# The row of reciprocals in a decoder step's RMS norms: products of a step-zero column with the identity in place of diagonal matrices

## The chip, the cores and the metric

The kernel runs on one core of a Trainium2 chip, as one launch. The metric is the device time of that launch in microseconds. Engines are named as in the profile: PE (TensorE's matmuls), PEld (its loads of a stationary operand, which run ahead of matmuls), DVE (VectorE), ACT (ScalarE), POOL (GpSimd) and SP (SyncE, which issues the DMAs here).

## The reference

One inference step of a decoder of two layers, for a prompt of 1024 tokens and for 8 x 8 sample tokens with their caches. The model width is 1024. Each layer has a mixer (layer 0: gated linear attention beside a convolution module; layer 1: dilated sliding-window attention beside a gated MLP) and a convolutional feed-forward network of 2 x 2816 columns; each of these four parts stands between two RMS norms.

```python
def rmsnorm(x, g):
    x32 = x.astype(jnp.float32)
    y = x32 * lax.rsqrt(jnp.mean(x32 * x32, axis=-1, keepdims=True) + EPS)
    return (y * g.astype(jnp.float32)).astype(x.dtype)
...
def trunk(x, ...):
    for layer in range(DEPTH):
        h = rmsnorm(x, p['norm_pre_mix'][layer])
        ...
        x = x + rmsnorm(y, p['norm_post_mix'][layer])
        h = rmsnorm(x, p['norm_pre_ffn'][layer])
        f, fb = conv_ffn(h, ffn_buf[layer], p['w_up'][layer], ...)
        x = x + rmsnorm(f, p['norm_post_ffn'][layer])
```

## The kernel before

**Layout and halves.** Activations lie transposed: the 1024 features on 8 tiles of 128 partitions, the tokens along the free dimension. The tokens are worked on in two halves. Half A has 512 tokens (4 blocks of 128); half B has 576 (4 blocks of 128 and the 64 sample tokens). A matrix product of half A has 512 moving columns, one of half B two pieces of 288.

**Products.** Each fp32 operand is split into a rounded part and a rest, and a product is three passes: `g<-hi,whi`, `g<-lo,whi` and `g<-hi,wlo`. A weight chunk is loaded as `raw`, ACT writes `whi`, DVE subtracts to get `wlo` (both with three buffers). `g` is a PSUM tile; ACT copies it out, or DVE adds it to `y`.

**A norm.** In the transposed layout a token's sum of squares runs over partitions. So PE multiplies the summed squares with a column of ones (`m<-ones,ss`), which gives one column per block of 128 tokens, with the tokens on partitions. DVE scales it (`r<-m`, L201, in `rstd`), POOL raises it to the power -1/2 (`r<-r,mhalf`, L236). The result `r` has a token on each partition, but the tiles to be scaled have tokens along the free dimension. `rb` turns the column into a row that is the same on all 128 partitions: for each block DVE writes a diagonal matrix `dg` (L201) and PE multiplies it with a matrix of ones (L230), which sums each column and so repeats the diagonal's values on every partition. ACT copies the PSUM tile to `rb` (L207); eight DVE operations `y<-y,vec,rb` (L198) scale the eight tiles; each is then split into `hi` (ACT) and `lo` (DVE), and the next matrix product reads these. `dg` has two buffers, so the third diagonal of a half can be written only when the first product has read its own.

There are 15 calls of `rb` in a launch (eight norms, each for two halves; half B's last one is done in another layout). The eight calls of half A have 4 blocks each, the seven of half B 5 blocks, which makes 67 diagonals and 67 products. In the trace each fp32 product is two matmul instructions and two loads. A name such as `m<-dg,ones` gives the output, then the moving operand, then the stationary one.

**The order of work.** The code issues work in program order, but a scheduler of the framework, which simulates a timeline, puts each engine's instructions in the order in which they are to run; an engine then keeps this order. So a change in a few instructions can move others on all engines. The matrix products of the other half, or of the part before, fill PE while a norm's chain runs.

Of the kernel before, what the change touches and what calls it, by code (L numbers as in the profile page):

```python
# [9 lines left out]
F32 = mybir.dt.float32  # L10
# [3 lines left out]
ALU = mybir.AluOpType  # L14
# [4 lines left out]
P = 128  # L19
# [119 lines left out]
class Kern:  # L139
# [292 lines left out]
    def rb(self, h, ss, r=None):  # L432

        nb = len(h.blocks)
        if r is None:
            ps = self.psn()
            for b, (c0, sz) in enumerate(h.blocks):
                for i, t in enumerate(ss):
                    self.mm(ps[:sz, b:b + 1], t[:, c0:c0 + sz], self.ones[:, :1], i == 0, i == len(ss) - 1)
            r = self.rms(h, ps)  # L440
        rb = self.np_.tile([P, h.n], F32, tag="rb", name=self.nm("rb"), bufs=1)
        for part in ([0, 1, 2, 3], [4]):
            if part[0] >= nb:
                continue
            pb = self.psn()
            for b in part:
                c0, sz = h.blocks[b]
                dg = self.np_.tile([P, P], F32, tag="dg", name=self.nm("dg"), bufs=2)
                self.ts(dg[:sz, :sz], self.ident[:sz, :sz], r[:sz, b:b + 1], 0.0, ALU.mult, ALU.add)
                o0 = c0 - h.blocks[part[0]][0]  # L450
                self.mm(pb[:, o0:o0 + sz], self.ones[:sz, :], dg[:sz, :sz], True, True)
            c0 = h.blocks[part[0]][0]
            w = sum(h.blocks[b][1] for b in part)
            self.acopy(rb[:, c0:c0 + w], pb[:, :w])
        return rb
# [8 lines left out]
    def pre_steps(self, h, xt, ss, name, l, out, r=None):  # L464
        rb = self.rb(h, ss, r)
        yield 1.0
        for k in range(KT):
            self.stt(xt[k], xt[k], self.v(name, l * KT + k), rb, ALU.mult, ALU.mult)
            out.append(self.split(h, xt[k]))
            yield 1.0  # L470

    def post_steps(self, h, y, ss, xs, name, l, xnew, out):
        xl = [self.at(h, [P, h.n], name="xl") for _ in range(KT)]
        for k in range(KT):
            self.dma(xl[k], xs[k])
        rb = self.rb(h, ss)
        yield 1.0
        ss2 = None
        for k in range(KT):
            self.stt(y[k], y[k], self.v(name, l * KT + k), rb, ALU.mult, ALU.mult)  # L480
            self.tt(y[k], y[k], xl[k], ALU.add)
            if xnew is not None:
                if ss2 is None:
                    ss2 = []
                self.sq_add(h, ss2, y[k], k)
                self.dma(xnew[k], y[k])
            yield 1.0
        out.append(ss2)
# [1532 lines left out]
```

## Time and profile before

| | |
|---|---|
| median of 3 runs | 2666.02 us (2665.92 to 2673.85) |
| profiled execution | 2670.34 us |
| its span | 2668.6 us |
| PE busy | 2572.5 us (96%) |
| DVE busy | 1750.3 us (66%) |
| ACT busy | 1210.0 us (45%) |
| POOL busy | 305.4 us (11%) |
| mean granted clock of TensorE | 0.979 |

The span is that of the trace; the profiled execution's own time has 1.7 us around it. Busy time of PE is modelled from overlapping instructions, so its share says how little of the span PE was without work, not how close it is to its peak. The granted clock is a share of 2.4 GHz.

### The profile page before, as it was taken

The page shows a single profiled execution, that of the slowest core. Times are in us where ns is not written, and L with a number is a line of the kernel's source. Part 1 is how long each engine was busy: PE and PEld are TensorE (multiplying, and loading weights), DVE is VectorE, ACT ScalarE, POOL GpSimd, SP SyncE. Part 2 cuts the span into 40 slices and gives each one's busy share as a digit, 9 for nine tenths or more (in the row PEclk, how much of TensorE's full clock was granted, in tenths as well). Part 3 has the DMA queues.
Part 4 walks back from the last instruction along what each step waited for, and adds up shares of the span by engine and source line. Part 5 has one row for each costly group of instructions (what it writes and reads, how often), then busy time and mean ns, then how long its engine had stood idle before and what let it go on. Part 6 is the DMA issues. An engine that isn't in the chain of part 4 may idle for free.

```text
span 2668.6 us, 43691 instructions
## 1 busy us (share of the span) xinstructions
PE 2572.5 (96%) x16481; PEld 2302.2 (86%) x16481; DVE 1750.3 (66%) x3298; ACT 1210.0 (45%) x2330; POOL 305.4 (11%) x594
## 2 busy tenths in 40 slices
PE   7999999999999999999999999889999898999998
PEld 6789788887888789999999889878877678999998
DVE  4888479999677546455558774666654478455556
ACT  5343455443455344535445452235552545434444
POOL 0100001201100001201204020010011112001100
PEclk9999999999999999999999999999998899999999
DMA  6433364455545544232332447875534154322232
GB/s 215 134 107 104 103 229 144 133 173 175 171 138 166 174 143 129 80 110 60 92 120 90 139 132 213 244 215 155 145 105 129 48 176 128 103 88 72 76 90 84
DMA packets 505002, 355.80 MB, mean 133 GB/s; under 512 B 29547, under 2 KB 461282, under 8 KB 504015
## 3 DMA queue, kind: packets, MB, share of 16 engines
q1 hardware_dynamic: 504791, 353.01, 44.1%
q8 instruction: 130, 2.13, 0.3%
q14 instruction: 81, 0.66, 0.1%
HBM read 306.43 MB, written 75.97 MB: 143 GB/s over the span
## 4 chain that ended last, share of the span: by engine, by line
PE 82%; DVE 6%; DMA 6%; ACT 3%; issue 2%; SPq 1%; POOL 0%; DVEq 0%; POOLq 0%; ACTq 0%
PE g L230 74%; PE m L230 6%; PE m L222 2%; DMA kc<-qr 2%; DVE wlo L195 1%; DVE y L198 1%; SPq L186 1%; DMA raw<-in_w_up 1%; ACT whi L207 1%; DMA kc<-in_cache_c_w 1%; DVE cv L198 1%; DVE y L195 1%; DMA raw<-in_w_down 1%; DVE w L195 0%; ACT S L210 0%
## 5 line engine op out<-in xcount | busy, mean ns | idle before, releaser
L230 PE MATMUL g<-hi,whi 128*128 128x288 f32 (+2 forms) x4440 | 1271.5, 334 | 20.4 <-ACT hi L207 6.2
L230 PE MATMUL g<-lo,whi 128*128 128x288 f32 (+2 forms) x4440 | 1264.7, 331 | 8.1 <-DVE lo L195 8.1
L230 PE MATMUL g<-hi,wlo 128*128 128x288 f32 (+1 forms) x4416 | 1251.0, 331 | 0.4 <-DVE wlo L195 0.4
L230 PEld LDWEIGHTS g<-hi,whi 128*128 128x128 f32 (+1 forms) x4440 | 770.6, 190 | 94.7 <-issue 9.5
L230 PEld LDWEIGHTS g<-lo,whi 128*128 128x128 f32 (+1 forms) x4440 | 772.3, 190 | 70.9 <-DVE lo L195 10.6
L207 ACT ACTIVATE whi<-raw 128x1024 fp32r<-128x1024 f32 (+3 forms) x478 | 413.1, 865 | 922.2 <-PE g L230 715.0
L230 PEld LDWEIGHTS g<-hi,wlo 128*128 128x128 f32 x4416 | 767.6, 190 | 62.1 <-issue 2.5
L195 DVE TENSOR_TENSOR wlo<-raw,whi 128x1024 fp32r<-128x1024 f32 (+2 forms) x476 | 468.1, 983 | 447.6 <-ACT whi L207 441.7
L198 DVE SCALAR_TENSOR_TENSOR c<-u,dw,c 128x512 f32<-128x512 f32 (+3 forms) x528 | 293.5, 591 | 57.9 <-ACT c L210 56.1
L210 ACT ACTIVATE c<-g,dw 128x288 f32<-128x288 f32 (+1 forms) x264 | 172.5, 656 | 2.3 <-DMA out_p_kv<-rows 1.3
L198 DVE SCALAR_TENSOR_TENSOR cv<-u,cvw,cv 128x512 f32<-128x512 f32 (+16 forms) x240 | 172.6, 734 | 1.2
L195 DVE TENSOR_TENSOR y<-y,g 128x288 f32<-128x288 f32 (+3 forms) x240 | 121.1, 525 | 71.4 <-PE g L230 70.9
L595 POOL COPY last<-u 128x2 f32<-128x2 f32 x88 | 82.5, 940 | 700.3 <-ACT u L207 700.3
L207 ACT ACTIVATE u<-g 128x224 f32<-128x224 f32 (+2 forms) x352 | 127.0, 392 | 25.8 <-PE g L230 20.6
L207 ACT ACTIVATE hi<-c 128x512 fp32r<-128x512 f32 (+1 forms) x88 | 57.7, 656 | 121.5 <-DVE c L195 121.3
L210 ACT ACTIVATE c<-c 128x512 f32<-128x512 f32 (+1 forms) x88 | 57.9, 658 | 98.3 <-DVE c L198 96.3
L612 POOL COPY lastp<-u 128x2 f32<-128x2 f32 x88 | 29.3, 333 | 464.9 <-ACT u L207 464.9
L195 DVE TENSOR_TENSOR lo<-c,hi 128x512 fp32r<-128x512 f32 (+1 forms) x88 | 63.3, 720 | 23.9 <-ACT hi L207 23.5
L236 POOL TENSOR_TENSOR r<-r,mhalf 128x4 f32<-128x4 f32 (+2 forms) x25 | 27.1, 1094 | 425.6 <-DVE r L201 425.6
L198 DVE SCALAR_TENSOR_TENSOR y<-y,vec,rb 128x512 f32<-128x512 f32 (+1 forms) x104 | 73.6, 774 | 0.6 <-ACT rb L207 0.5
L210 ACT ACTIVATE sq<-y 128x512 f32<-128x512 f32 (+3 forms) x107 | 64.8, 621 | 14.1 <-DVE ss L195 7.1
L195 DVE TENSOR_TENSOR ss<-ss,sq 128x512 f32<-128x512 f32 (+1 forms) x91 | 64.8, 717 | 8.9 <-ACT sq L210 8.3
(281 smaller groups left out, 1963.7 us busy)
## 6 DMA issues: line engine op xcount, KB each, us to landing
raw<-in_w_up SPq DMA_DIRECT2D x176, 512.0 KB
raw<-in_w_down SPq DMA_DIRECT2D x128, 256.0 KB
raw<-in_w_in_odd SPq DMA_DIRECT2D x44, 512.0 KB
raw<-in_w_in_even SPq DMA_DIRECT2D x40, 512.0 KB
out_s_kv<-in_cache_c_w SPq DMA_DIRECT2D x32, 512.0 KB
raw<-in_w_down SPq DMA_DIRECT2D x64, 192.0 KB
xl<-x SPq DMA_DIRECT2D x40, 256.0 KB
kc<-in_cache_c_w SPq DMA_DIRECT2D x80, 128.0 KB
```

Source lines behind the costliest of these rows:

```text
L186: self.nc.sync.dma_start(out, in_)
L195: self.nc.vector.tensor_tensor(out=out, in0=a, in1=b, op=op)
L198: self.nc.vector.scalar_tensor_tensor(out=out, in0=a, scalar=s, in1=b, op0=op0, op1=op1)
L207: self.nc.scalar.activation(out, in_, AF.Copy, scale=scale)
L210: self.nc.scalar.activation(out, in_, func, **kw)
L222: self.nc.tensor.transpose(out, in_, self.ident[:k, :k])
L230: self.nc.tensor.matmul(out, l, r, start=start, stop=stop)
L236: self.nc.gpsimd.tensor_tensor(out=out, in0=out, in1=self.mhalf[:p, :n], op=ALU.pow)
L595: self.nc.gpsimd.tensor_copy(self.last2[l][:, jt, :], u[:, 512:514])
L612: self.nc.gpsimd.tensor_copy(self.lastp[:, :, jt], u[:, 512:514])
```

## The change

The diagonals go. The stationary operand of each product is now the column `r[:, b]` itself, read with a step of zero so that it stands 128 times side by side, and the moving operand is the identity. The result in PSUM has the same shape and place. Nothing else in the code differs.

```diff
             pb = self.psn()
             for b in part:
                 c0, sz = h.blocks[b]
-                dg = self.np_.tile([P, P], F32, tag="dg", name=self.nm("dg"), bufs=2)
-                self.ts(dg[:sz, :sz], self.ident[:sz, :sz], r[:sz, b:b + 1], 0.0, ALU.mult, ALU.add)
                 o0 = c0 - h.blocks[part[0]][0]
-                self.mm(pb[:, o0:o0 + sz], self.ones[:sz, :], dg[:sz, :sz], True, True)
+                self.mm(pb[:, o0:o0 + sz], r[:sz, b:b + 1].to_broadcast([sz, P]), self.ident[:sz, :sz], True, True)
             c0 = h.blocks[part[0]][0]
             w = sum(h.blocks[b][1] for b in part)
             self.acopy(rb[:, c0:c0 + w], pb[:, :w])
```

On DVE exactly the 67 operations `dg<-ident,r` are missing. On PE the number of products is the same. But the scheduler's order moves. In the program's names below, `m_...` is the PSUM tile of a norm, `g_...` that of a matrix product, and the numbers count tiles (they differ between the kernels).

**First place: PE, the norm of half A ahead of the input product of layer 1's mixer** (about 850 us in the trace of before). Rows of before: the four products of the norm stand directly ahead of the first matrix product that reads the norm's result (`hi_7941`), with only the sums of another norm between.

```order
L230 MATMUL g_8451<-hi_8008,wlo_8447 128x288
L230 MATMUL g_8452<-hi_8008,wlo_8447 128x288
L230 MATMUL m_7926<-dg_7927,ones 128x128
L230 MATMUL m_8526<-w_1672_8521,w_1667_8517 4x384
L230 MATMUL m_7926<-dg_7930,ones 128x128
L230 MATMUL m_7926<-dg_7933,ones 128x128
L230 MATMUL m_7926<-dg_7936,ones 128x128
...
L230 MATMUL g_8513<-hi_7941,whi_8508 128x512
L230 MATMUL g_8617<-hi_7941,whi_8612 128x512
```

Rows of the change: the four products (`m_7884`) stand together, 39 matrix products of half B ahead of the first that reads the norm's result (`hi_7891`).

```order
L230 MATMUL g_8401<-lo_7935,whi_8396 128x288
L230 MATMUL m_7884<-ident,r_7880 128x128 x4
L230 MATMUL g_8402<-lo_7935,whi_8396 128x288
L230 MATMUL g_8401<-hi_7934,wlo_8397 128x288
L230 MATMUL g_8402<-hi_7934,wlo_8397 128x288
...
L230 MATMUL g_8401<-hi_7958,wlo_8397 128x288
L230 MATMUL g_8402<-hi_7958,wlo_8397 128x288
L230 MATMUL g_8463<-hi_7891,whi_8458 128x512
L230 MATMUL m_8476<-w_1647_8471,w_1642_8467 4x384
L230 MATMUL g_8557<-hi_7891,whi_8552 128x512
```

What moved: 39 matrix products now stand between the row's making and its first reader, where there were none.

**Second place: PE, the norm of half B ahead of the same mixer's input product, while down products of half A (`128x512`) run** (about 1570 us). Before, the products come in pairs, as the two buffers of the diagonals allow: two, 20 matrix products, two, 20 matrix products, the one of 64 tokens, and 20 matrix products later the first reader (`hi_15857`).

```order
L230 MATMUL g_16177<-hi_16037,wlo_16173 128x512
L230 MATMUL m_15828<-dg_15829,ones 128x128
L230 MATMUL m_15828<-dg_15832,ones 128x128
L230 MATMUL g_16197<-hi_15696,whi_16192 128x512
...
L230 MATMUL m_15828<-dg_15835,ones 128x128
L230 MATMUL m_15828<-dg_15838,ones 128x128
L230 MATMUL g_16217<-hi_15935,wlo_16213 128x512
...
L230 MATMUL m_15842<-dg_15843,ones 128x64
L230 MATMUL g_16257<-lo_15803,whi_16252 128x512
...
L230 MATMUL g_16298<-hi_15857,whi_16293 128x288
```

Of the change: all five stand together, and 83 matrix products lie between them and the first reader (`hi_15751`).

```order
L230 MATMUL g_16031<-hi_15931,wlo_16027 128x512
L230 MATMUL g_16051<-hi_15600,whi_16046 128x512
L230 MATMUL m_15732<-ident,r_15726 128x128 x4
L230 MATMUL m_15738<-ident,r_15726 128x64
L230 MATMUL g_16051<-lo_15601,whi_16046 128x512
...
L230 MATMUL g_16171<-lo_15932,whi_16166 128x512
L230 MATMUL g_16171<-hi_15931,wlo_16167 128x512
L230 MATMUL g_16192<-hi_15751,whi_16187 128x288
L230 MATMUL g_16193<-hi_15751,whi_16187 128x288
```

What moved: 20 matrix products between the last of these products and the reader have become 83.

**Third place: DVE, the norm of half B ahead of its up product in layer 1, again beside down products of half A** (about 2210 us). Before: the eight `y<-y,vec,rb` stand behind the weights' rests (`wlo`) of the running down product.

```order
L195 TENSOR_TENSOR wlo_22589<-raw_22587,whi_22588 128x1024
L577 COPY fst<-m_22202 128x64
L577 COPY fst<-m_22235 128x64
L195 TENSOR_TENSOR ss_22445<-ss_22445,sq_22544 128x512
L198 SCALAR_TENSOR_TENSOR y_21604<-y_21604,vec,rb_22174 128x576
L198 SCALAR_TENSOR_TENSOR y_21641<-y_21641,vec,rb_22174 128x576
...
L198 SCALAR_TENSOR_TENSOR y_21831<-y_21831,vec,rb_22174 128x576
L198 SCALAR_TENSOR_TENSOR y_21869<-y_21869,vec,rb_22174 128x576
L195 TENSOR_TENSOR wlo_22703<-raw_22701,whi_22702 128x1024
L195 TENSOR_TENSOR y_16130<-y_16130,g_22573 128x512
L577 COPY fst<-m_22282 128x64
...
L195 TENSOR_TENSOR lo_22213<-y_21604,hi_22212 128x576
```

Of the change: the eight stand ahead of `lo_22299`, which the running down product of half A needs, and ahead of the adds `y_16017<-y_16017,g_22308` and of `wlo_22363`.

```order
L195 TENSOR_TENSOR c_22251<-c_22251,c_22289 128x512
L575 COPY fst<-m_22076 128x64
L575 COPY fst<-m_22109 128x64
L198 SCALAR_TENSOR_TENSOR y_21498<-y_21498,vec,rb_22058 128x576
L198 SCALAR_TENSOR_TENSOR y_21535<-y_21535,vec,rb_22058 128x576
...
L198 SCALAR_TENSOR_TENSOR y_21725<-y_21725,vec,rb_22058 128x576
L198 SCALAR_TENSOR_TENSOR y_21763<-y_21763,vec,rb_22058 128x576
L195 TENSOR_TENSOR lo_22299<-c_22251,hi_22298 128x512
L195 TENSOR_TENSOR lo_22087<-y_21498,hi_22086 128x576
L575 COPY fst<-m_22156 128x64
...
L195 TENSOR_TENSOR y_16017<-y_16017,g_22308 128x512
L195 TENSOR_TENSOR wlo_22363<-raw_22361,whi_22362 128x384
```

What moved: a train of eight operations has gone ahead of work that PE waits for.

## Rows read from the trace of the kernel before

**Rows 1.** The page: busy time of the engines, and the chain that ended last.

```profile
PE 2572.5 (96%) x16481; PEld 2302.2 (86%) x16481; DVE 1750.3 (66%) x3298; ACT 1210.0 (45%) x2330; POOL 305.4 (11%) x594
PE 82%; DVE 6%; DMA 6%; ACT 3%; issue 2%; SPq 1%; POOL 0%; DVEq 0%; POOLq 0%; ACTq 0%
```

**Rows 2.** The diagonals, all of them: ns minimum/median/maximum; DVE's idle time before them.

```profile
L230 PE MATMUL m<-dg,ones x134: 270/275/377, 18.5 to 2238.3; 128*128 128x128 f32 x120, 64*128 64x64 f32 x14
L201 DVE TENSOR_SCALAR dg<-ident,r x67: 241/284/290, 12.8 to 2235.1; 128x128 f32<-128x128 f32 x60, 64x64 f32<-64x64 f32 x7
  POOL r L236: 12.9, 12
```

**Rows 3.** Loads of a stationary operand by shape: busy us, mean ns, idle before.

```profile
L230 PEld LDWEIGHTS m<-dg,ones 128*128 128x128 f32 x120 | 17.8, 190 | 3.8 <-DVE dg L201 2.3
L230 PEld LDWEIGHTS m<-w,v 128*64 128x64 f32 x240 | 13.6, 141 | 6.4 <-issue 5.3 <-ACT w L207 0.6 <-DVE w L218 0.4
L230 PEld LDWEIGHTS m<-kp,q 64*128 64x128 f32 x40 | 5.7, 206 | 4.6 <-issue 3.7 <-DVE stat L1537 0.4
```

**Rows 4.** Timeline 850 to 867: start, us, instructions, [idle before <- its releaser].

```profile
850.63 0.95 PE L230 MATMUL m<-ones,ss 128*128 128x1 f32 x8
859.38 0.49 PE L230 MATMUL m<-dg,ones 128*128 128x128 f32 x2 [1.33 <-DVE dg L201]
859.91 0.60 ACT L207 ACTIVATE rb<-m 128x512 f32<-128x512 f32 x1 [1.31 <-PE m L230]
860.54 5.39 DVE L198 SCALAR_TENSOR_TENSOR y<-y,vec,rb 128x512 f32<-128x512 f32 x8 [0.54 <-ACT rb L207]
862.01 1.22 PE L230 MATMUL g<-hi,whi 128*128 128x512 f32 x3 [0.64 <-ACT hi L207]
866.58 0.80 PE L230 MATMUL g<-lo,whi 128*128 128x512 f32 x1 [3.35 <-DVE lo L195]
```

**Rows 5.** The chain that ended last: two unbroken stretches of matrix products.

```profile
1115.64 5.58 PE g L230 x42
1517.12 4.56 PE g L230 x20
```

**Rows 6.** Windows of two stretches; columns up to PEclk, the granted clock.

```profile
862.60:872.70 10.10, 6.75 (x16) 4.84 (x15) 8.75 (x18) 3.80 (x7) 5.54 (x2) 0.50 0.54 169
1586.20:1593.00 6.80, 6.08 (x25) 6.08 (x26) 6.48 (x9) 2.25 (x4) 0.00 (x0) 0.50 0.69 209
```

**Rows 7.** Timeline 1577 to 1588, PE.

```profile
1577.43 0.43 PE L230 MATMUL m<-dg,ones 64*128 64x64 f32 x2
1585.07 0.40 PE L230 MATMUL g<-hi,whi 128*128 128x288 f32 x1 [2.06 <-ACT y L207]
1586.92 0.85 PE L230 MATMUL g<-lo,whi 128*128 128x288 f32 x2 [1.45 <-DVE lo L195]
```

**Rows 8.** PE's waits, 2184 to 2226: us, times, longest; and one DVE row there.

```profile
PE g L230 <- DVE y L195: 3.2, 1, 3.2
PE g L230 <- ACT hi L207: 2.2, 2, 1.3
PE m L222 <- DMA w<-in_state_ffn_conv: 2.1, 2, 1.3
2210.26 5.91 DVE L198 SCALAR_TENSOR_TENSOR y<-y,vec,rb 128x576 f32<-128x576 f32 x8
```

**Rows 9.** PE's waits in 365 to 389 (first row) and 1444 to 1496.

```profile
PE m L222 <- ACT hi L207: 2.6, 1, 2.6
PE g L230 <- DVE y L195: 2.8, 3, 1.4
```

**Rows 10.** Timeline 852 to 873: POOL's powers, and DVE beside the second pair.

```profile
852.27 1.01 POOL L236 TENSOR_TENSOR r<-r,mhalf 128x4 f32<-128x4 f32 x1 [34.88 <-DVE r L201]
866.59 4.28 DVE L195 TENSOR_TENSOR lo<-y,hi 128x512 fp32r<-128x512 f32 x7
866.75 5.54 POOL L236 TENSOR_TENSOR r<-r,mhalf 128x4 f32<-128x4 f32 x2 [13.46 <-DVE r L201]
```

## The prediction

> **What bounds the kernel now.** The page is read first: PE is busy for 96% of the span and holds 82% of the chain that ended last [rows 1]. So time is won only where PE stands idle or runs at its lower clock, and DVE's work counts only where PE waits for it. Next come the rows on the diagonals themselves [rows 2]: 134 instructions of 275 ns on PE, 67 of 284 ns on DVE. Then the timeline at the norms, which shows what PE waits for behind the row of reciprocals [rows 4, 7 to 9], and last the granted clock of the stretches behind such waits [rows 6]. To price what is moved I use unbroken stretches: 42 matmuls of half B in 5.58 us, 0.133 us each, and 20 of half A in 4.56 us, 0.228 us each [rows 5].
>
> **What the change removes.** 60 operations of 284 ns and 7 of some 245 ns, together 18.8 us of DVE. DVE is not the bound, so by itself that is worth nothing. It also takes away DVE's 12.9 us of idling for POOL before the diagonals [rows 2], which is off the path too.
>
> **What it adds.** The products stay as many and as large, so PE's busy time is taken as unchanged. New is that a stationary operand is read with step zero; no row shows such a load. The loads of 128 columns that there are take 141 to 206 ns on average whatever is read, and those of the old products 190 [rows 3]. I take 190. From below: 50 ns less on 134 loads would give 6.6 us if all of it were exposed, which a load ahead of its matmul is not. From above: a load twice as long, all exposed, costs 134 x 0.19 = 25.5 us. The nearest rows lie all within 16 ns above 190, so I stay at nothing and keep the upper end as a rival.
>
> **What it moves** carries the forecast. The pairs are gone, all products of a call stand together, and behind them the whole chain starts sooner.
>
> *First place (layer 1's mixer, half A).* In the trace the fourth product comes at 859.38, 8.8 us after the sums began at 850.63. From its end at 859.87 it takes 6.7 us to the first product on `lo` at 866.58: the copy 0.60, eight scalings 5.39, one `lo` [rows 4]. PE's idle time there is 1.33 + 0.64 + 3.35 = 5.3 us. In the new order 39 matmuls of half B (5.2 us) stand between products and reader, then three products on `hi` and one small product (1.1 us) ahead of the first on `lo`: 6.3 us of cover for 6.7. So 0.4 us stays and 4.9 go. Behind the idle time the stretch 862.6 to 872.7 ran at granted clock 0.50, that is 1.2 GHz, with 6.75 us of PE work [rows 6]; at 2.4 GHz it would take 3.4 us less. Whether the clock still falls I can't tell, so I take half, 1.7. Term: 6.6 (4.9 to 8.3).
>
> *Second place (the same mixer, half B).* From the last product at 1577.43 (0.43 long) to the first on `lo` at 1586.92 are 9.1 us, with 2.06 + 1.45 us of idle time [rows 7]. In the new order 83 matmuls of half A, 18.9 us, lie between products and reader in place of 20. Both waits go: 3.5 us. The scalings stand ahead of a weight's `wlo` whose reader comes 40 matmuls (9.1 us) behind the products; that covers a copy, eight scalings and three operations just so. Half of the lower clock behind it, 6.08 / 2 = 3.0, adds 1.5. Term: 5.0 (0 to 6.5).
>
> *Third place (layer 1's up product, half B).* Here the order turns against the kernel. Before, PE idles 3.2 + 2.2 + 2.1 = 7.5 us around the eight scalings [rows 8], which now go. But the scalings (5.91 us) now stand ahead of `lo_22299`. Between the norm's products and the reader of that `lo` PE has nine matmuls of half A (2.1 us) and five groups of small transposes, some 1.6 us: 3.7 of cover. The chain is two copies of some 0.8 together, scalings 5.91, `lo` 0.7, so 7.4: a new wait of 3.7 us. Then eight `lo` of 0.7 us, copies and an add stand ahead of `wlo_22363`, some 7.5 us, and PE reaches its reader ten matmuls (2.3 us) after the one before: a second new wait of about 5. Term: 7.5 - 9 = -1.5, taken as -2, since hand-overs are not counted in the new waits (-8 if the waits for the transposes' tiles stay besides and grow, +7.5 if DVE keeps pace).
>
> *Elsewhere.* In 1444 to 1496 PE waits 2.8 us for `y` on DVE, which has fewer operations to do now; I take half, 1.4 (0 to 2.8). In 365 to 389 it waits 2.6 us for `hi` [rows 9]; the row comes earlier there, but the copies between two groups of transposes now stand behind the eight scalings, so I take 0 (-3 to 3). Other regions are reordered a little: 0, some 4 either way.
>
> *The wait that moves.* DVE used to stand between POOL and PE. Now PE waits for POOL itself, and behind a waiting product all of PE's queue stands. From the end of the sums at 851.58 to the end of the power at 853.28 are 1.7 us [rows 4, 10]. In 13 calls (all but the first norm's) 16 to 38 matmuls, 3.6 to 5.9 us, lie between sums and products in the new order, so some 2 us are to spare. But with DVE in a run of seven `lo` beside it, a pair of powers took 5.54 us [rows 10]. Until now DVE waited for the power ahead of its diagonals and so left it alone; now it goes on working. In seven of the calls four to six operations (some 2.4 to 3.6 us) follow the scaling of the sums on DVE; held for all of these, the power would make PE wait in the four of them with the shortest cover, 0.8 to 1.4 us each. I take -1 in all (0 to -5).
>
> The Trainium skill, page "SBUF — State Buffer", section "SBUF: two separate sides", says that a DVE operation with two SBUF inputs and a GpSimd operation that reads SBUF lock each other out for the whole of an instruction. By that rule the 5.54 us beside 1.01 us are no accident, the sum would take the -5, and the forecast would stand at 2660.
>
> **Sum.** 6.6 + 5.0 - 2 + 1.4 + 0 - 1 = 10 us less. From the profiled execution's 2670.3 that is 2660.3; that execution was 4.3 us above the median, so from 2666.0 it gives **2656 us**. A measurement of this kernel tells a change from none at about 0.3%, 8 us: below 2658 is faster, above 2674 slower.
>
> **Rivals.**
> *The waits only move* (2665). For it: trains of eight scalings stand earlier on DVE at all places, and at the third PE waits at once for what is behind them. If that term is -8 and both clocks still fall (-3.2), 10 - 6 - 3.2 leaves 0.8. Against it: at the first and second place the cover is counted and long.
> *POOL's power becomes what PE waits for* (slower, 2680). If DVE holds every power as long as the one in rows 10, 4.0 us over the usual 1.0, PE waits 4.0 - 2.1 = 1.9 us in each of 13 calls, 25 us instead of 1: 2656 + 24 = 2680. It decides, that is, makes the kernel slower by over 8 us, from some 10 calls on. For it: the row itself. Against it: in six calls at most three operations follow on DVE before the scalings, and these wait for the row, so that DVE leaves POOL alone.
> *The step-zero load is dearer* (slower, up to 2681). It decides from 18 / 134 = 0.14 us more on each load. For it speaks only that no row shows one; against it, that the rows of all shapes lie so close.
> *More comes back* (2645). The clock doesn't fall at either place (+3.2) and DVE keeps pace at the third (+7.5 instead of -2).
>
> **How the numbers follow.** Forecast 0.47, waits only move 0.25, a few powers held (2661) 0.08, powers held throughout 0.06, dearer load 0.06, more comes back 0.08. The forecast's own range is 2649 to 2663, and nearly a tenth of the whole lies in its upper part, past 2658: faster 0.47 - 0.07 + 0.08 = 0.48. Slower takes both slower rivals and a little of the first, 0.14; no change is left with 0.38. The range runs from 2644, where more comes back, to 2671, past the waits that only move; outside lie the slower cases and some 0.04 below.
>
> **What would show it.** Right: no operation `dg` on DVE; loads of the new products at 190 ns; at the first place no wait of over 1 us for `lo`, at the second none for `y` or `lo`; at the third new waits for `lo` and `wlo` of 4 and 5 us. PE's waits for `r` on POOL together under 5 us. Wrong, if loads of `r` take over 0.3 us, if PE waits for POOL in most calls, if the clock falls in new places, or if the reordered regions between the norms, which I put at zero, show waits of their own.

## The result, and the profile after

The change makes the kernel faster: 2650.07 us median of 5 runs (2648.64 to 2656.84), against 2667.61 us for the kernel before in the same comparison (2665.92 to 2674.22). The ratio is 0.9944, with a 95% interval of 0.9929 to 0.9959: 15 us less by the ratio, 17.5 by the medians. The profiled executions, on which what follows rests, are 2670.34 and 2650.05 us, 20.3 us apart.

The page of the kernel after, busy time by engine and the chain that ended last:

```profile
PE 2567.3 (97%) x16481; PEld 2298.6 (87%) x16481; DVE 1738.2 (66%) x3231; ACT 1211.5 (46%) x2331; POOL 282.9 (11%) x594
PE 85%; DMA 6%; DVE 4%; ACT 2%; issue 1%; SPq 1%; POOL 0%; DVEq 0%; POOLq 0%; ACTq 0%
```

PE has the same 16481 instructions and is busy for 5.2 us less [rows 1], though no product went; the windows below show that this is mostly TensorE's granted clock. The other 15 us are idle time of PE. The rows on the tile `r` give the new products and loads (ns: minimum/median/maximum):

```profile
L230 PEld LDWEIGHTS m<-ident,r x134: 182/190/192, 18.1 to 2215.7; 128*128 128x128 f32 x120, 64*128 64x128 f32 x14
L230 PE MATMUL m<-ident,r x134: 270/275/347, 18.1 to 2215.8; 128*128 128x128 f32 x120, 64*128 64x64 f32 x14
L236 POOL TENSOR_TENSOR r<-r,mhalf x25: 534/1012/1461, 11.5 to 2641.8; 128x4 f32<-128x4 f32 x15, 64x1 f32<-64x1 f32 x8, 128x2 f32<-128x2 f32 x2
```

A load with step zero takes what the old loads took, 190 ns, and a product 275 ns [rows 2, 3].

At the first place the rows of [rows 4] from the norm's products on now read like this, with the DVE row of `lo` beside them (the kernel after, timeline of PE, ACT and DVE):

```profile
850.92 1.05 PE L230 MATMUL m<-ident,r 128*128 128x128 f32 x8
852.01 0.60 ACT L207 ACTIVATE rb<-m 128x512 f32<-128x512 f32 x1
852.74 5.38 DVE L198 SCALAR_TENSOR_TENSOR y<-y,vec,rb 128x512 f32<-128x512 f32 x8
857.00 0.40 PE L230 MATMUL g<-hi,whi 128*128 128x512 f32 x1
858.04 3.09 DVE L195 TENSOR_TENSOR lo<-y,hi 128x512 fp32r<-128x512 f32 x5
858.78 0.50 PE L230 MATMUL g<-lo,whi 128*128 128x512 f32 x1
```

No row has idle time in brackets: PE reaches `lo` 6.8 us after the products' end, when the first of the five `lo` is just done.

To see where the time came from, both spans are cut at the same matrix products (counted along PE's `g` rows). The windows view of the kernel before, from the first product to 137 us, then to 451, the first place, the waits of [rows 9] that lie behind 1465 us, the second place, and from 2145 to shortly ahead of the end, which holds the third place (columns: length, then busy time of PE, PEld, DVE, ACT and POOL with their instructions, the granted clock, and two on the DMA):

```profile
24.60:137.00 112.40, 111.18 (x487) 88.46 (x487) 79.57 (x119) 44.42 (x69) 11.07 (x10) 0.97 0.54 155
137.00:451.40 314.40, 299.38 (x1988) 268.34 (x1987) 244.27 (x474) 152.58 (x288) 20.99 (x24) 0.98 0.43 133
849.00:973.70 124.70, 117.51 (x543) 94.28 (x542) 70.89 (x115) 49.81 (x75) 8.65 (x6) 0.95 0.57 170
1465.20:1515.60 50.40, 47.62 (x312) 44.42 (x311) 37.68 (x74) 20.74 (x33) 5.03 (x5) 1.00 0.51 153
1515.60:1612.40 96.80, 93.29 (x483) 81.14 (x482) 65.50 (x96) 49.40 (x83) 19.29 (x10) 0.96 0.43 130
2145.40:2657.10 511.70, 500.64 (x3599) 486.05 (x3598) 312.33 (x550) 232.29 (x468) 62.91 (x187) 0.99 0.33 99
```

And the same stretches of the kernel after:

```profile
23.70:133.30 109.60, 108.23 (x488) 86.76 (x486) 80.66 (x117) 44.96 (x70) 6.49 (x10) 1.00 0.55 162
133.30:450.90 317.60, 303.52 (x1989) 269.86 (x1988) 240.90 (x464) 154.04 (x289) 23.50 (x24) 0.97 0.42 132
849.70:960.50 110.80, 110.80 (x535) 90.30 (x534) 67.30 (x100) 49.03 (x75) 4.08 (x5) 1.00 0.62 192
1453.40:1500.60 47.20, 47.05 (x312) 44.25 (x312) 32.44 (x63) 19.65 (x30) 3.03 (x4) 1.00 0.52 160
1500.60:1593.90 93.30, 91.06 (x484) 78.66 (x483) 63.98 (x88) 49.54 (x83) 9.48 (x10) 1.00 0.44 133
2124.60:2636.80 512.20, 501.52 (x3599) 487.16 (x3598) 310.38 (x536) 233.69 (x468) 57.09 (x187) 0.99 0.33 99
```

Length less PE's busy time is idle time. The first place gives 13.9 us: 7.2 of idle time, all there was, and 6.7 of busy time, of which the lower clock is most (0.95 against 1.00); the rest is a group of eight sums that the window before still holds. The two next give 3.2 and 3.5 us. From the third place on nothing is won (0.5 lost). The beginning gives 2.8 and the stretch after it takes 3.2, both mostly by the clock: PE's instructions are the same to one, its busy time falls by 2.9 and grows by 4.1. All the rest of the span gives 0.6.

Each window is of one execution. The change and six of the runs below have the same order in the beginning, in the stretch after it, and at the second place. Cut at the same products, the stretch after the beginning takes 316.8 to 318.0 us in these seven and the second place 92.9 to 94.4, so that loss and that gain come each time. The beginning takes 109.0 to 112.6, so its gain does not.

What PE waits for at the second place and at the third in the kernel after (1500.6 to 1593.9 the first two rows; 2124.6 to 2237.7 the others):

```profile
PE g L230 <- ACT whi L207: 1.8, 2, 1.3
PE g L230 <- DVE wlo L195: 0.5, 1, 0.5
...
PE m L222 <- DMA w<-in_state_ffn_conv: 3.6, 3, 1.6
PE g L230 <- DVE y L195: 2.8, 1, 2.8
PE g L230 <- DVE lo L195: 1.8, 1, 1.8
PE g L230 <- DVE wlo L195: 1.3, 2, 0.9
```

At the second place the waits for `y` and `lo` [rows 7] are gone, and 2.3 us for weights have come. At the third the waits of [rows 8] are replaced by others: with the shorter waits that neither list shows, the place's window has 9.4 us of idle time before and 10.6 after. The wait for the loads of the state, 2.1 us before, has grown to 3.6.

### The profile page after: what moved, and what is told of

Same layout as the page of the kernel before. It is cut to its first block, busy times and chain, and to the rows that moved or that the text cites. A ratio compares the mean times of both kernels' runs of the same rounds, so it can differ in the third digit from the quotient of the medians.

```text
span 2648.3 us, 43633 instructions
## 1 busy us (share of the span) xinstructions
PE 2567.3 (97%) x16481; PEld 2298.6 (87%) x16481; DVE 1738.2 (66%) x3231; ACT 1211.5 (46%) x2331; POOL 282.9 (11%) x594
## 4 chain that ended last, share of the span: by engine, by line
PE 85%; DMA 6%; DVE 4%; ACT 2%; issue 1%; SPq 1%; POOL 0%; DVEq 0%; POOLq 0%; ACTq 0%
PE g L230 75%; PE m L230 7%; PE m L222 2%; DMA kc<-qr 2%; DMA raw<-in_w_down 1%; DVE wlo L195 1%; DMA raw<-in_w_up 1%; DMA kc<-in_cache_c_w 1%; SPq L186 1%; ACT whi L207 1%; DVE y L198 0%; ACT S L210 0%; DVE cv L198 0%; ACT L210 0%; DMA out_p_kv<-rows 0%
## 5 line engine op out<-in xcount | busy, mean ns | idle before, releaser
L198 DVE SCALAR_TENSOR_TENSOR cv<-u,cvw,cv 128x512 f32<-128x512 f32 (+21 forms) x240 | 174.9, 739 | 2.2 <-ACT cv L210 0.5
L593 POOL COPY last<-u 128x2 f32<-128x2 f32 x88 | 73.9, 841 | 715.2 <-ACT u L207 715.2
L207 ACT ACTIVATE u<-g 128x224 f32<-128x224 f32 (+2 forms) x352 | 126.7, 391 | 20.6 <-PE g L230 17.5
L610 POOL COPY lastp<-u 128x2 f32<-128x2 f32 x88 | 35.4, 402 | 494.0 <-ACT u L207 494.0
L195 DVE TENSOR_TENSOR c<-c,c 128x512 f32<-128x512 f32 (+1 forms) x88 | 63.4, 721 | 1.3
```

What stands on the lines that cost most here:

```text
L195: self.nc.vector.tensor_tensor(out=out, in0=a, in1=b, op=op)
L198: self.nc.vector.scalar_tensor_tensor(out=out, in0=a, scalar=s, in1=b, op0=op0, op1=op1)
L207: self.nc.scalar.activation(out, in_, AF.Copy, scale=scale)
L593: self.nc.gpsimd.tensor_copy(self.last2[l][:, jt, :], u[:, 512:514])
L610: self.nc.gpsimd.tensor_copy(self.lastp[:, :, jt], u[:, 512:514])
```

## The experiments

All ratios are to the kernel before, taken on the same chip in the same comparison.

**Is it DVE's time or the place in the order?** In the kernel of the change DVE writes the diagonals all the same, and nobody reads them:

```diff
+                dg = self.np_.tile([P, P], F32, tag="dg", name=self.nm("dg"), bufs=2)
+                self.ts(dg[:sz, :sz], self.ident[:sz, :sz], r[:sz, b:b + 1], 0.0, ALU.mult, ALU.add)
                 o0 = c0 - h.blocks[part[0]][0]
                 self.mm(pb[:, o0:o0 + sz], r[:sz, b:b + 1].to_broadcast([sz, P]), self.ident[:sz, :sz], True, True)
```

> The kernel of the change, in which DVE still writes all 67 diagonals, that nobody reads; the products stay those of the step-zero column, and every engine's order is that of the change but for the 67 operations. Theory (what gains is the place of the products in PE's order, so that the row is ready earlier; DVE's time is off the path): as the change, 2646 to 2657 us, ratio to the kernel before 0.992 to 0.997. Rival (the gain comes from DVE's 18.8 us of work and its 12.9 us of waiting for POOL): the gain goes, 2663 to 2670 us.

Measured: 2649.41 us, ratio 0.9937 (0.9924 to 0.9949). The rows of the diagonals in this run, with DVE's idle time before them:

```profile
L201 DVE TENSOR_SCALAR dg<-ident,r x67: 241/281/328, 13.2 to 2213.1; 128x128 f32<-128x128 f32 x60, 64x64 f32<-64x64 f32 x7
  POOL r L236: 12.3, 11
```

The 67 operations and the 12.3 us of waiting for POOL are back, and the kernel is as fast as the change. So DVE's time was worth nothing and the rival falls. What gains is in the order of the work, which this run shares with the change; which parts of the order, the next runs ask.

**The same without the new read.** In the kernel before, the diagonals get other numbers of buffers, four or one in place of two:

```diff
-                dg = self.np_.tile([P, P], F32, tag="dg", name=self.nm("dg"), bufs=2)
+                dg = self.np_.tile([P, P], F32, tag="dg", name=self.nm("dg"), bufs=4)
```

> The kernel before with four buffers for the diagonals in place of two, so that four products of a call can stand together, with ones as stationary operand and no read with step zero. In its order the first place has 6 matrix products between the norm's products and their reader (0 before, 39 in the change), the second 52 behind the fifth product (20 before, 83 in the change). Theory: it gains where it stands earlier, that is at the second place (3 us) and little at the first (0 to 3 us): 2655 to 2664 us. Rival (DVE's time): no change, 2664 to 2670 us. A second rival (the step-zero read itself gains): no change either.

Measured: 2654.56 us, ratio 0.9962 (0.995 to 0.9975), at the edge of what the theory gave and beyond both rivals. So two more buffers alone give some two thirds of the gain. In its profile the gain does not come from the two expected places alone: the first gives 3.9 us and the second 2.5, the stretch behind 1465 us gives 3.8 (46.6 us, no idle time), and from the third place on 6.3 are won, while the stretch from 137 to 451 us loses 5.8. At the first place the products stand 6 matrix products earlier, but PE's waits for `hi` and `lo` are no shorter (1.3 and 4.5 us, 0.6 and 3.4 before), so what the first place gains does not come from them.

> The kernel before with one buffer for the diagonals in place of two: each product stands some 20 matrix products behind the one ahead of it, so a row is ready later still. Work is the same. Theory: slower than the kernel before by 4 to 15 us, 2671 to 2682 us, with longer waits for what stands behind the row. Rival (DVE's time): no change, 2664 to 2670 us.

Measured: 2693.56 us, ratio 1.0103 (1.009 to 1.0116), slower by more than expected. PE now waits for the diagonals themselves (the first rows of PE's waits in this run, whole span):

```profile
PE m L230 <- DVE dg L201: 18.4, 13, 3.8
...
PE g L230 <- ACT hi L207: 11.1, 7, 2.3
PE g L230 <- DVE lo L195: 8.8, 4, 3.7
```

The wait for `dg` was 1.3 us with two buffers, and the expectation had only the waits behind the row in it. The granted clock of this run's whole span is 0.974, against 0.979 in the kernel before, so part of the loss is clock.

**One place alone: does the cover explain the first place, and the clock?** In the kernel of the change the reciprocals of that one call are held back on POOL by four or twelve multiplications. The reader stays where it is, so the products move towards it. The scheduler's order changes with them from about 850 to 950 us and in a few products around 2085 us; in the run with four it also changes between 2190 and 2260 us, at and behind the third place, which the expectation did not have.

```diff
             r = self.rms(h, ps)
+        for _ in range(hold):
+            self.nc.gpsimd.tensor_scalar(out=r[:, :4], in0=r[:, :4], scalar1=1.0, scalar2=0.0, op0=ALU.mult, op1=ALU.add)
```

> The kernel of the change, in which POOL multiplies the reciprocals of the one call at the first place four times by 1, so that they are ready later; 30 matrix products lie between that call's products and their reader in place of 39, all other places as in the change. Theory (cover: 6.7 us of chain behind the products against the matrix products and some 1.1 us of first passes): cover 4.0 + 1.1 = 5.1, so PE idles some 1.6 us there (0 in the change), and the granted clock stays at 1.00: 2650 to 2654 us. Rival (what waited there before had another cause than the lateness of the row): no idle time, 2648 to 2652 us.

> As the run before, with twelve multiplications: 13 matrix products lie between products and reader. Theory: cover 1.7 + 1.1 = 2.8 us, so some 3.9 us of idle time for hi and lo there. Two theories on the clock: if it falls behind such idle time, as in the kernel before, the place loses 2 to 5 us more than its idle time, 2655 to 2660 us in all; if the lower clock there had another cause, it loses the idle time alone, 2653 to 2656 us.

Measured: 2648.86 us, ratio 0.994 (0.9915 to 0.9965), and 2655.98 us, ratio 0.9968 (0.9955 to 0.998). The totals decide little. The first lies in the rival's range and under the theory's; the second lies in both ranges, where the two theories on the clock overlap. The windows of the place itself decide. The first place, between the same products as above, in the run with four multiplications, then with twelve, then in the kernel before with four diagonals:

```profile
851.00:964.40 113.40, 111.50 (x535) 90.08 (x533) 67.38 (x100) 48.49 (x75) 3.59 (x5) 1.00 0.62 187
```

```profile
854.80:973.60 118.80, 113.92 (x535) 91.95 (x534) 67.22 (x100) 48.73 (x75) 6.47 (x13) 0.97 0.58 179
```

```profile
853.90:974.70 120.80, 113.88 (x542) 92.09 (x541) 70.50 (x115) 49.03 (x75) 5.22 (x6) 0.97 0.57 176
```

With 39, 30, 13, 6 and 0 matrix products between the norm's products and the reader, PE idles in this window for 0, 1.9, 4.9, 6.9 and 7.2 us. Not all of that is this norm's. For 30 the forecast was 1.6 us; only 0.5 of the 1.9 is the wait for `lo`, the rest are short waits elsewhere in the window, so the totals agree by chance. For 13 the waits for `hi` and `lo` were put at 3.9 together; they are 4.9. PE's waits in the window of the run with four (the first row), then of the run with twelve:

```profile
PE g L230 <- DVE lo L195: 0.5, 1, 0.5
...
PE g L230 <- DVE lo L195: 3.9, 1, 3.9
PE g L230 <- ACT hi L207: 1.0, 1, 1.0
```

So a later row brings these waits back, within about 1 us of the count. With 6 and with 0 products in between they are 5.8 and 5.3 us (the latter with the wait for `dg` [rows 4]), so they no longer grow there.

The clock goes with the idle time: 1.00, 1.00, 0.97, 0.97 and 0.95 in the five runs. In the run with twelve it fell at 867.2 us, in the middle of the wait for `lo` that ended at 868.85 (windows view):

```profile
867.20:874.00 6.80, 5.15 (x12) 4.09 (x13) 6.48 (x10) 1.22 (x3) 0.00 (x0) 0.50 0.64 187
```

Its busy time at the place is 2.4 us longer than in the run with four for the same 535 instructions, at the low end of the 2 to 5 expected. Over all the runs here it is the same: in the six with 0 to 1.9 us of idle time at this place (the change, the idle diagonals, four multiplications, and the three runs below) the granted clock is 1.00, in the four with 4.9 us or more it is 0.93 to 0.97. So idle time there brings the lower clock. Elsewhere the clock also varies without such a cause: the beginning, up to 137 us, has the change's order in the run with twelve and no more idle time (0.8 us, 1.4 in the change), and yet a clock of 0.95 where the change has 1.00.

**The third place.** Four tiles in turn in place of two for the loads of the state, which are transposed between the matrix products there:

```diff
-            rw = self.wk(1 + g % 2, [16, 512])
+            rw = self.wk(1 + g % (4 if l else 2), [16, 512])
```

> The kernel of the change with four tiles in turn in place of two for the loads of layer 1's state of the feed-forward convolution, so that a load needn't wait for the transposes of the tile two ahead; all orders nearly as in the change. Theory (part of the third place's waits is those loads): PE's three waits for them, 3.6 us, go, 2644 to 2649 us, 2 to 5 us under the change. Rival (DVE's train of eight scalings is what ends last there): the waits for y and lo grow by as much, no change, 2649 to 2653 us.

Measured: 2648.59 us, ratio 0.9931 (0.9917 to 0.9946); not to be told from the change. PE's waits at the third place of this run:

```profile
PE g L230 <- DVE lo L195: 3.3, 1, 3.3
PE g L230 <- DVE y L195: 2.7, 1, 2.7
PE g L230 <- DVE wlo L195: 1.5, 2, 1.0
```

The 3.6 us for the loads are gone, and the wait for `lo` behind the scalings has grown from 1.8 to 3.3. Both sides hold in part: the loads were what ended last before the transposes, and less than half of their wait comes back behind them.

Then the calls of `rb` from the third place on go back to diagonals, in four buffers, which puts their products later. `self.diag` is set ahead of half B's two norms around that place and stays set. So the last call, half A's at about 2212 us, has diagonals too, 14 in all, although the expectation speaks of half B's two norms alone:

```diff
+                if self.diag:
+                    dg = self.np_.tile([P, P], F32, tag="dg", name=self.nm("dg"), bufs=4)
+                    self.ts(dg[:sz, :sz], self.ident[:sz, :sz], r[:sz, b:b + 1], 0.0, ALU.mult, ALU.add)
+                    self.mm(pb[:, o0:o0 + sz], self.ones[:sz, :], dg[:sz, :sz], True, True)
+                    continue
```

> The kernel of the change, with diagonals in four buffers kept in the two norms of half B at the third place alone; there the products stand where they do with four diagonals (15 and 33 matrix products later in all than in the change), elsewhere all is as in the change. Theory (at the third place the row of the change comes too early for DVE's queue, and its train of scalings stands ahead of what PE waits for): the place takes some 104 us, as with four diagonals, in place of 113: 2640 to 2646 us. Rival (what four diagonals gained there came from what lies ahead of it in that kernel): no change against the change, 2648 to 2653 us.

> As the run before, and with four tiles in turn for the loads of layer 1's state. If these loads still end last at the third place: 1 to 4 us under the run before, 2638 to 2645 us. If the later scalings have given the loads time already: as the run before.

Measured: 2645.51 us, ratio 0.9932 (0.9908 to 0.9955), and 2645.14 us, ratio 0.9929 (0.9906 to 0.9952). The first lies in the theory's range and under the rival's; the second is as the run before. By the ratios they are 3 and 4 us under the change, but the intervals overlap with the change's 0.9929 to 0.9959. In the window from the third place on, the run without and then the run with the tiles read:

```profile
2125.00:2630.30 505.30, 499.77 (x3599) 485.35 (x3598) 312.53 (x550) 232.08 (x468) 56.96 (x187) 0.99 0.34 100
```

```profile
2123.10:2630.40 507.30, 499.90 (x3600) 485.14 (x3599) 312.49 (x550) 232.48 (x468) 57.64 (x187) 0.99 0.34 100
```

The kernel before with four diagonals has 505.4 there, and the five runs with the products of the change at this place 508.4 (four tiles alone) to 512.2. The means are 506.0 and 510.0, so the later products are worth some 4 us in this window, less than expected, and on top of them the tiles give nothing more. Whether the total beats the change stays open at that size, and so does which of the three calls gives the 4 us.

## Why the prediction was right, and where its terms were off

The forecast was 10 us less, 2656 us with a range of 2644 to 2671; the median is 2650.07, 16 less than the 2666.0 that the forecast set out from. Direction and mechanism hold: the products of a call stand together, the row is ready earlier, and PE's idle time behind the late row goes. That the sum came out as near as it did is in part luck, since terms that were too small and losses that were not foreseen offset each other. The terms, each against the lengths of the windows above:

- **Step-zero load, priced at nothing.** Right: 182 to 192 ns. That rival is closed by the profile. (The 141 ns in the term's reading of [rows 3] is a load of 64 columns; those of 128 are the 190 and the 206.)
- **DVE's work, priced at nothing.** Right, shown by the run with idle diagonals.
- **First place, 6.6 us (4.9 to 8.3).** 13.9 came in its window: this term was furthest off. At the norm itself all 5.3 us of idle time went, where 4.9 were forecast, and the stretch at 1.2 GHz behind it [rows 6] went whole, 3.4 us, where half was entered. That makes 8.7, a little past the term's upper end; the half was the step that was mis-sized. Most of the other 5 us lie in the same window, where the term did not look: before, the sums of other norms waited 1.8 us for DVE, and a second stretch at 1.2 GHz, 3.4 us long, began 2 us after the longest of these waits (the kernel before, timeline and windows view):

```profile
921.95 1.23 PE L230 MATMUL m<-ones,ss 128*128 128x1 f32 x10 [1.54 <-DVE ss L195]
924.00:927.40 3.40, 3.40 (x10) 2.63 (x9) 1.14 (x5) 0.34 (x1) 1.56 (x2) 0.50 0.83 233
```

  Both are gone, and a group of sums of 0.95 us [rows 4] now lies outside the window. Why the sums no longer wait was not tried. The runs that bring this norm's idle time back bring part of the lower clock back.
- **Second place, 5.0 us.** 3.5 came: 1.3 of idle time, where 3.5 were forecast, and 2.2 of busy time by the clock, where 1.5 were. Both waits went and the clock came back to 1.00 in full, but there are 2.3 us of new waits for weights; the term had taken the `wlo` (0.5) as just covered and did not have the `whi` (1.8).
- **1444 to 1496, 1.4 us.** 3.2: the waits for `y` went altogether. The reason that the term gave, fewer operations on DVE, fails. In the run with idle diagonals, where DVE has these operations, the stretch has no idle time either (windows view of that run), and so it is in the kernel before with four diagonals. It was the order.

```profile
1456.50:1503.10 46.60, 46.60 (x312) 44.22 (x311) 33.48 (x68) 19.75 (x30) 3.07 (x4) 1.00 0.53 162
```

- **Third place, -2 us.** -0.5 from there on, but not by the term's parts. Of the 7.5 us of waits that were to go, the one for the loads of the state, 2.1, stayed and grew to 3.6, as in the term's lower case. The new waits behind the train of scalings are of the kind foreseen and smaller: `lo` 1.8 us for 3.7, `wlo` 1.3 for 5, and a wait for `y` of 2.8 that wasn't named. That the row came too early there is borne out by the runs with later products, which shorten the stretch.
- **365 to 389, 0 us.** The stretch of 137 to 451 around it lost 3.2 us, by the clock. Why the clock falls there longer than before was not tried.
- **POOL, -1 us.** PE waits for POOL's powers nowhere; the longest power is 1.46 us. That rival is closed for this order. By the Trainium skill's rule on locked ports, "SBUF — State Buffer", "SBUF: two separate sides", the term was -5. Three of the 25 powers began beside a DVE operation that was under way, and took 1.45, 1.04 and 1.46 us; each time it was a single operation, so the rule had little to act on. In two things the runs differ from that rule: a power was held for a whole run of operations and not for one, and a `wlo` that began beside a power was not held by it (both in the last section).

Of the rivals, "the waits only move" held at the third place alone. "More comes back" was right on the clock at the first and second place and wrong on the third, where DVE did not keep pace; it was given 0.08, and its own terms add up to 2643, not 2645. One sign of being wrong did show: the clock fell in places where it had not fallen before, from 1094.2, 1933.9 and 2145.5 us on, for 3.4, 3.4 and 6.8 us. Why was not tried.

## What to carry to other kernels

An operation off the bounding engine can still set where the scheduler puts what follows it: here two buffers of a small tile spread five products over some 40 matrix products, and four buffers alone gave two thirds of what the new formulation gave. Count, at each place, the work of the bounding engine between the making of a value and its first reader, against the chain between them; that count gave the waits at one place within about 1 us in three kernels (39, 30 and 13 products in between). Idle time removed ahead of a dense stretch can bring the clock back as well, so the lower-clock stretches behind a wait belong to its price. And earlier need not be better where the freed work runs ahead of something the bounding engine needs sooner: at the third place later products took some 4 us off a stretch of 510, though the totals do not tell the kernels apart.

## What the runs showed of the hardware

A power of 128 rows on POOL takes 1.0 us when nothing holds it, one of 64 rows 0.5. It is held by DVE operations with two inputs in SBUF that are under way when it starts. In the run with one diagonal it started 0.17 us into a run of three `lo`, each of 0.7 us, and took 2.8 us, ending 0.9 us after the last of them (POOL and DVE of that run):

```profile
2246.83 2.09 DVE L195 TENSOR_TENSOR lo<-y,hi 128x576 fp32r<-128x576 f32 x3
2247.00 2.80 POOL L236 TENSOR_TENSOR r<-r,mhalf 128x4 f32<-128x4 f32 x1 [25.36 <-DVE r L201]
```

It was held for the whole run of these operations, as by the seven `lo` of [rows 10], not for one. A copy out of PSUM that was under way did not hold it: in the run with four diagonals the power at 925.84 took 1.01 us beside one. Nor did an operation that began well after the power. In the kernel after, a power of 128 rows began at 914.84 and took 1.01 us, though a `wlo` started beside it at 915.23; the `wlo` took 1.23 us, no more than others of its size (1.22 us at 850.75, 1.20 at 861.51). The power of 64 rows behind it began when that `wlo` was under way and took 1.04 us; the one at 1496.63, with DVE idle, took 0.54 (timelines of POOL and DVE, windows cut so that each power has its own row):

```profile
914.84 1.01 POOL L236 TENSOR_TENSOR r<-r,mhalf 128x4 f32<-128x4 f32 x1 [43.38 <-DVE r L201]
915.23 1.23 DVE L195 TENSOR_TENSOR wlo<-raw,whi 128x1024 fp32r<-128x1024 f32 x1 [0.41 <-ACT whi L207]
915.83 1.04 POOL L236 TENSOR_TENSOR r<-r,mhalf 64x1 f32<-64x1 f32 x1
1496.63 0.54 POOL L236 TENSOR_TENSOR r<-r,mhalf 64x1 f32<-64x1 f32 x1
```
